# A fused mixer step on Trainium2: the opening of the kernel rewritten as one written order for all engines

## The chip, the cores and the metric

The kernel runs on one core of one Trainium2 chip. The metric is the device time of one execution in microseconds (us), lower is better. The engines of the core run side by side, each with its own queue: PE multiplies matrices, DVE (VectorE) and ACT (ScalarE) work element by element, POOL (GpSimd) does so more slowly, and SP issues the transfers from memory (DMA).

## The reference, cut to what matters

One layer of a mixer for 1024 prompt tokens and 32 sample tokens, width 1024. Everything that follows the opening hangs on `hn`:

```python
mod = jax.nn.silu(c) @ p['w_ada'] + p['b_ada']
shift, scale, gate = jnp.split(mod, 3, axis=-1)
hn = rmsnorm(x, p['norm_g']) * (1.0 + scale[:, None]) + shift[:, None]
proj = hn @ p['w_in']
lru_x, lru_g, xbc, z, dt_raw = jnp.split(proj, ...)
...
xbc_c, new_buf_ssd = causal_conv(xbc, buf_ssd, p['ssd_conv_w'], p['ssd_conv_b'])
xbc_c = jax.nn.silu(xbc_c).astype(jnp.float32)
xs, Bm, Cm = jnp.split(xbc_c, [D_SSD, D_SSD + SSD_GROUPS * SSD_STATE], axis=-1)
dt = jax.nn.softplus(dt_raw + p['ssd_dt_bias'])
```

Then come a chunked state-space scan over 16 heads, a gated linear recurrence (LRU) of width 1024, an output projection and a last RMS norm. There is a prompt row and a sample row of `c`, so every shift, scale and gate has two columns.

## The kernel before, in words

**Tiling.** Features lie on the 128 partitions and tokens along the free dimension. The tokens form three blocks of 384, 384 and 290 columns; the last holds 256 prompt tokens, 32 sample tokens and two columns that carry the shift. A *unit* is 128 output columns of a weight matrix, all 1024 inputs deep, loaded as 8 k-tiles of 128 x 128 (512 KB). Each fp32 operand of a projection is split into a high and a low part, so that a unit takes three matmuls per k-tile and block: high weight x high h (line 219), high weight x low h (220), low weight x high h (221). That is 24 matmuls per block and 72 per unit. `split_unit` makes the parts of a weight: a cast on ACT (line 95) and a subtraction on DVE (97), once on POOL. Units 24 and 25 are the two groups of B, 26 and 27 those of C, 16 to 23 the eight head pairs of x, 28 to 35 those of z.

**The opening** (lines 272 to 372) makes h and with it the first projections:

- The SP queue loads, in the order `XLOAD`: x in pieces (`x`: four for block 0, two each for blocks 1 and 2), w_ada in single units (`s`), the weights of dt (`w`), units 24 and 25 (`B`, `C` in the order of the string).
- `load_x` squares each piece on ACT (line 170) and adds the squares, on DVE for block 0 and on POOL for blocks 1 and 2 (174, 176). `sum_x` and `token_rstd` sum over the features with matmuls against ones (131), take the root on ACT (135) and invert on DVE (136). `norm_x` spreads the result over the partitions with matmuls against the identity (141), copies it to SBUF (186) and scales x with it: five k-tiles of block 0 on DVE from PSUM (192), all others on POOL (194).
- `ada_unit` multiplies silu(c) with one unit of w_ada (eight fp32 matmuls in four column groups, line 114), copies the row out (115) and `ada_columns` turns rows into columns with the selector `sel` (120). Eight units give the scale (`a`, `c` and Acol in line 302), eight more the shift (`s`, lines 364 to 368).
- `h_new` makes, for each k-tile as soon as x is scaled and Acol is there, the high part of h on ACT (210, the *head*) and the low part on DVE (211, the *tail*).
- PE and SP follow the string `PROG`: `W` is a warm-up matmul on ones (289), `a`, `c`, `r`, `R`, `s` as above, `p` and `q` one k-tile of unit 24 and of unit 25, `d` the dt projection of a block (266). The string holds 33 `W`, 16 `p` and 16 `q`, after the 8 warm-up matmuls of `WARM`. It is followed by the shift, the dt block 2 and the last block of unit 24.

The order of DVE, ACT and POOL in the opening, and that of everything behind it, is chosen by the scheduler of the kernel language from its own timeline.

**Behind the opening.** dt is transposed (382); `b_post(0)` and `b_post(1)` move a unit to SBUF with the shift bias (line 238), convolve it (one ACT pass, line 417, and three DVE passes, 419), apply silu and transpose (515); unit 25's last block is projected in between; `dt_chain` works out the decays and writes them to memory; `c_post` does the same for units 26 and 27 and forms the masked C x B products (527, 531). Then come unit 16 and a loop over eight head pairs with two units each (`ssd_decay` scans on DVE, line 551; `ssd_tokens` 567, 569; `ssd_states` 583, 592; `ssd_diag` with the yd matmuls, 608), the LRU loop and the output projection.

## Time and profile before

| What | us |
|---|---|
| Median of three runs (785.03 to 786.59) | 786.38 |
| The profiled execution | 786.8 |
| Its span, from the first to the last instruction | 785.1 |
| First matmul of a projection (line 219) | 20.39 |
| Last matmul of unit 24 | 75.06 |
| First yd matmul of head pair 0 | 146.31 |

How to read the profile lines. A stretch (`10.00:20.00 ...`) gives its length, then for each engine the us in which it was busy and the number of its instructions, then the granted clock of PE (1.00 is full speed), the busy share of the DMA engines and GB/s. A row in order of time gives the start, the duration, engine, line, operation, the tile written and the tiles read, the count, and in brackets the idle time of the engine before it with what ended it. A grouped row ends in `xcount | busy us, mean ns | idle us before, by what`. A row of waits gives total us, times, longest. PEld is PE's loading of weights, which runs beside its matmuls. The modelled duration of a matmul is longer than the step from one to the next; steps are what counts for PE.

### The profile page before, as it was taken

What the parts mean: (1) busy time and instruction counts of PE and PEld (TensorE: products, weight loads), DVE (VectorE), ACT (ScalarE), POOL (GpSimd) and SP (SyncE); (2) the same over time, 40 slices, a digit from 0 to 9 for tenths busy, and PEclk for the clock granted to TensorE, in tenths of its full rate; (3) what the DMA queues carried; (4) which work ended last, traced back from release to release, by engine and by line L of the source; (5) the groups of instructions that cost most, each with busy time, mean ns of one, the idle gap of its engine ahead of it and who ended that gap; (6) DMA issues with size and microseconds to landing.
All of it is one profiled execution on the core that took longest, in us unless ns stands there. A gap on an engine that the chain in (4) does not pass through costs nothing.

```text
span 785.1 us, 13046 instructions
## 1 busy us (share of the span) xinstructions
PE 761.6 (97%) x5230; PEld 737.0 (94%) x5230; DVE 534.5 (68%) x842; ACT 415.2 (53%) x609; POOL 78.0 (10%) x179
## 2 busy tenths in 40 slices
PE   8899999999999999999999999999999999999994
PEld 7678999989999999998999999999999999999994
DVE  3575966798887787877475566546658897635643
ACT  6553855335244253443578877886777654323430
POOL 3581211001000000000010011101101000000000
PEclk9899999999999999999999999999999999999997
DMA  9920214244433424342212111111153685744831
GB/s 326 395 101 2 78 40 139 88 134 139 137 110 121 147 63 161 116 122 89 78 66 88 43 61 35 54 34 61 31 150 114 191 276 162 236 138 142 262 111 68
DMA packets 40188, 96.32 MB, mean 123 GB/s; under 512 B 4536, under 2 KB 22208, under 8 KB 40128
## 3 DMA queue, kind: packets, MB, share of 16 engines
q1 hardware_dynamic: 40128, 95.50, 37.7%
q8 instruction: 41, 0.67, 0.3%
q14 instruction: 19, 0.16, 0.1%
HBM read 85.53 MB, written 9.95 MB: 122 GB/s over the span
## 4 chain that ended last, share of the span: by engine, by line
PE 80%; DVE 9%; DMA 5%; ACT 2%; issue 2%; POOL 1%; SPq 0%; POOLq 0%; DVEq 0%; ACTq 0%
PE pj L221 16%; PE pj L219 16%; PE pj L220 16%; PE mix L862 6%; PE mix L860 6%; PE mix L861 6%; PE yd L608 2%; PE dS L583 2%; DVE hb L211 2%; DMA M<-dA_d 2%; DVE wlo L97 1%; DMA sraw<-in_w_ada_dram 1%; PE yo L623 1%; DVE M L551 1%; PE gt L744 1%
## 5 line engine op out<-in xcount | busy, mean ns | idle before, releaser
L220 PE MATMUL pj<-hb,whi 128*128 128x384 f32 (+1 forms) x864 | 282.8, 327 | 2.5 <-DVE hb L211 2.5
L219 PE MATMUL pj<-hb,whi 128*128 128x384 f32 (+1 forms) x864 | 284.6, 329 | 0.0
L221 PE MATMUL pj<-hb,wlo 128*128 128x384 f32 (+1 forms) x864 | 282.4, 327 | 1.2 <-POOL wlo L97 1.2
L220 PEld LDWEIGHTS pj<-hb,whi 128*128 128x128 f32 x864 | 163.3, 189 | 4.2 <-DVE hb L211 3.2
L221 PEld LDWEIGHTS pj<-hb,wlo 128*128 128x128 f32 x864 | 163.6, 189 | 3.1 <-POOL wlo L97 1.6
L219 PEld LDWEIGHTS pj<-hb,whi 128*128 128x128 f32 x864 | 162.7, 188 | 3.2 <-issue 2.9
L95 ACT CAST whi<-wraw 128x1024 fp32r<-128x1024 f32 x84 | 88.0, 1048 | 142.3 <-PE pj L220 69.4
L97 DVE TENSOR_TENSOR wlo<-wraw,whi 128x1024 fp32r<-128x1024 f32 x83 | 102.5, 1236 | 59.3 <-ACT whi L95 59.3
L862 PE MATMUL mix<-yt,wlo 128*128 128x324 f32 (+2 forms) x320 | 103.9, 326 | 1.0 <-DVE wlo L97 1.0
L860 PE MATMUL mix<-yt,whi 128*128 128x324 f32 (+2 forms) x320 | 104.1, 325 | 0.0
L861 PE MATMUL mix<-yt,whi 128*128 128x324 f32 (+2 forms) x320 | 103.7, 324 | 0.0
L419 DVE SCALAR_TENSOR_TENSOR u<-raw,par,u 128x1060 f32<-128x1060 f32 x60 | 79.7, 1328 | 1.6 <-ACT u L417 1.1
L862 PEld LDWEIGHTS mix<-yt,wlo 128*128 128x128 f32 x320 | 60.0, 188 | 1.4 <-DVE wlo L97 1.3
L860 PEld LDWEIGHTS mix<-yt,whi 128*128 128x128 f32 x320 | 60.1, 188 | 0.2
L861 PEld LDWEIGHTS mix<-yt,whi 128*128 128x128 f32 x320 | 60.0, 188 | 0.1
L238 ACT ACTIVATE raw<-pj,sb 128x384 f32<-128x384 f32 (+2 forms) x80 | 33.9, 477 | 23.0 <-PE pj L221 13.3
L551 DVE TENSOR_TENSOR_SCAN M<-M,mask 128x1060 f32<-128x1060 f32 x16 | 37.8, 2363 | 11.8 <-DMA M<-dA_d 11.8
L879 DVE SCALAR_TENSOR_TENSOR ot<-mix,gate,xr 128x352 f32<-128x352 f32 (+3 forms) x32 | 14.8, 489 | 25.4 <-PE mix L862 21.5
L405 POOL COPY cso<-raw 128x3 f32<-128x3 f32 x20 | 11.8, 590 | 195.9 <-ACT raw L238 195.9
L211 DVE SCALAR_TENSOR_TENSOR hb<-x,Acol,hb 128x384 fp32r<-128x384 f32 (+2 forms) x32 | 28.0, 925 | 3.8 <-ACT hb L210 3.8
L756 DVE SCALAR_TENSOR_TENSOR r<-a,r 128x1060 f32<-128x1060 f32 x8 | 10.1, 1264 | 28.2 <-ACT r L755 28.2
L554 ACT ACTIVATE M<-M 128x1060 f32<-128x1060 f32 x16 | 17.5, 1091 | 22.2 <-DVE M L551 20.3
(228 smaller groups left out, 1063.5 us busy)
## 6 DMA issues: line engine op xcount, KB each, us to landing
wraw<-in_w_out_dram SPq DMA_DIRECT2D x48, 512.0 KB, 3.6
wraw<-in_w_in_dram SPq DMA_DIRECT2D x36, 512.0 KB, 3.7
M<-dA_d SPq DMA_DIRECT2D x16, 530.0 KB, 4.9
sraw<-in_w_ada_dram SPq DMA_DIRECT2D x16, 512.0 KB, 10.2
E<-E_d SPq DMA_DIRECT2D x16, 265.0 KB, 4.0
yz_d<-y SPq DMA_DIRECT2D x8, 530.0 KB, 4.2
wraw<-in_w_ada_dram SPq DMA_DIRECT2D x8, 512.0 KB, 4.4
x<-in_xh_dram SPq DMA_DIRECT2D x4, 384.0 KB, 4.8
```

The source lines that it names most:

```text
L95: nc.scalar.copy(hi, raw)
L97: eng.tensor_sub(lo, raw, hi.bitcast(F32))
L211: nc.vector.scalar_tensor_tensor(hb[b][:, k, 1, s:e], x[:, s:e], Acol[:, k, w:w + 1], hi.bitcast(F32), op0=OP.mult, op1=OP.subtract)
L219: nc.tensor.matmul(out, lhsT=hi[:, kk, :], rhs=hh, start=(kk == 0), stop=False)
L220: nc.tensor.matmul(out, lhsT=hi[:, kk, :], rhs=hl, start=False, stop=False)
L221: nc.tensor.matmul(out, lhsT=lo[:, kk, :], rhs=hh, start=False, stop=(kk == KT - 1))
L238: nc.scalar.activation(dst[0:P, off + d:off + d + e - s], banks[b][0:P, s:e], func, bias=sb[0:P, w:w + 1])
L419: nc.vector.scalar_tensor_tensor(u, raw[:, k:k + TW], wcol(k), u, op0=OP.mult, op1=OP.add)
L551: nc.vector.tensor_tensor_scan(M, M, mask, 0.0, op0=OP.add, op1=OP.mult)
L860: nc.tensor.matmul(ps, lhsT=w[0][:, k, :], rhs=yh, start=(half == 1 and k == 0), stop=False)
L861: nc.tensor.matmul(ps, lhsT=w[0][:, k, :], rhs=yl, start=False, stop=False)
L862: nc.tensor.matmul(ps, lhsT=w[1][:, k, :], rhs=yh, start=False, stop=(half == 0 and k == KT - 1))
```

## The change

The strings `XLOAD` and `PROG` give way to two lists, and the opening (lines 272 to 372) is rewritten so that SP, PE, ACT, DVE and POOL all follow the written order. The list was found by simulating a list schedule, outside of the kernel.

- Three units (24, 25, 26) go through the opening side by side, k-tile by k-tile: a token `m b k u` multiplies both weight parts of unit u with the head of h (two matmuls), `t b k u` the high part with the tail (one matmul). All three blocks of the three units are done when the opening ends.
- w_ada is loaded and multiplied in pairs of units (`s`), with three buffers of two units where there were six of one.
- All sums of squares (`a`, `f`) and all scaling of x (`x`, from PSUM, two k-tiles at a time) are on DVE. POOL is left with memsets and small copies.
- The other tokens: `z` n warm-up matmuls, `q` squares, `c` sums, `r` root, `v` inverse, `b` spreading, `o` copy of a row pair, `k` columns, `A` Acol (on DVE), `h` head, `l` tail, `H` and `L` the two parts of a weight, `p` parks a finished block in SBUF (ACT) so that its PSUM bank comes free, `d` and `e` half a dt block and its copy, `w` and `W` the parts of the dt weights, `K` and `S` the shift, `D` and `E` dt block 2, `y` finishes a unit: block 2 goes to SBUF with the bias, and DVE adds the bias to the 768 parked columns.
- Behind the opening `b_post` and `c_post` take the finished rows, and unit 27 is projected as before. Its loads and those of unit 16 are issued behind the last load of the opening.

```diff
-WARM = 8
-XP = (4, 2, 2)
-SR = 6
-POOL_K = (3, 5, 6)
-XLOAD = "xxxxsxsCsBssswxsxsxssssssss"
-PROG = ("WWWWWWWWWaWWWWWWraWRWcWaWWWWWWcWWWWqpaWWWaqcaqWp"
-        "aWcqppapqcrqqRppdqprpqsqpRqppssqpqqpsssppqssdq")
+FIRST = (24, 25, 26)
+LOADS = "x00 x02 x04 x06 w s w s w s x10 x14 s d s s s s x20 x24".split()
+PROG = (
+        "z34 q00 q02 a02 q04 a04 q06 H0 a06 f0 L0 c0 s0 r0 v0 b0 o0 H1 k0 x00 A0 L1 h00 z6 s2 A1 l00 h01 m000 "
+        "m001 x02 H2 t000 t001 m010 l01 m011 o2 k2 L2 t010 t011 s4 A2 A3 h02 x04 m002 h03 m020 t002 l02 m021 o4 "
+        "m012 q10 l03 t020 t021 t012 k4 q12 x06 m022 q14 m030 A4 t022 A5 m031 a12 h04 t030 m032 t031 h05 m040 l04 "
+        "t032 q16 m041 a14 s6 w l05 t040 t041 o6 m042 W a16 k6 t042 m050 A6 m051 A7 h06 f1 t050 m052 h07 t051 l06 "
+        "c1 l07 t052 m060 r1 m061 v1 t060 b1 t061 m062 x10 m070 t062 m071 x12 h10 t070 m072 p00 t071 s8 l10 p01 "
+        "h11 x14 m100 m101 o8 t072 h12 t100 l11 t101 s10 p02 l12 h13 x16 m102 o10 m110 m111 q20 l13 t102 t110 q22 "
+        "t111 m112 m120 q24 a22 m121 q26 t112 t120 a24 t121 m122 h14 m130 a26 m131 h15 t122 l14 t130 h16 t131 "
+        "m132 l15 m140 h17 m141 l16 t132 t140 t141 l17 m142 m150 f2 m151 c2 t142 t150 r2 t151 m152 v2 b2 m160 x20 "
+        "m161 t152 t160 x22 t161 h20 m162 m170 x24 h21 m171 s12 x26 h22 t162 s14 l20 o12 h23 l21 m172 o14 t170 "
+        "t171 t172 h24 l22 K d10 d11 e1 d00 d01 e0 p10 l23 p11 l24 p12 h25 S h26 l25 h27 l26 l27 m200 t200 m210 "
+        "t210 m220 t220 m230 t230 m240 t240 m250 t250 m260 t260 m270 t270 y0 D E m201 t201 m211 t211 m221 t221 "
+        "m231 t231 m241 t241 m251 t251 m261 t261 m271 t271 y1 m202 t202 m212 t212 m222 t222 m232 t232 m242 t242 "
+        "m252 t252 m262 t262 m272 t272 y2 "
+).split()
...
+    def scale_x(b, k):
+        w = XB[b][1]
+        x = xin[b][:, k:k + 2, :]
+        nc.vector.tensor_mul(x, x, xbc[b][:, None, 0:w].to_broadcast([128, 2, w]))
...
+    with tc.manual_schedule(engines={E.SP, E.PE, E.Activation, E.DVE, E.Pool}):
...
         def load_next():
+            t = left_loads[0]
+            if t == "s":
+                n = len(sraw)
+                if n >= 3 and 2 * n - 6 not in paired:
                     return False
+                sraw.append(st.tile([128, 2, KT, 128], F32, name="sraw", tag="sraw", bufs=3))
+                u = (2 * n + KT) % (2 * KT)
+                last[0] = dma(sraw[n], a["w_ada"][u:u + 2].rearrange("i p k n -> p i k n"))
+            elif t == "w":
+                ws.append(fetch_unit(a["w_in"][FIRST[len(ws)]]))
+            elif t == "d":
+                dma(wdt, a["w_dt"])
+            else:
+                if t == "x20" and "l07" not in seen:
+                    return False
+                last[0] = load_x(int(t[1]), int(t[2]))
...
+        def mm(u, b, k, heads):
+            w = ws[u]
+            for i in range(2) if heads else (0,):
+                nc.tensor.matmul(banks[u][b], lhsT=w[i][:, k, :], rhs=hb[b][:, k, 0 if heads else 1, :],
+                                 start=(heads and k == 0 and i == 0), stop=(not heads and k == KT - 1))
...
+        def park(u, b):
+            if u not in raws:
+                raws[u] = raw_tile(FIRST[u] - 8, ssd_state(FIRST[u] - 16), ("raw", "raw", "zs")[u])
+            for (s, e, d, w) in EV[b]:
+                nc.scalar.copy(raws[u][:, 3 + d:3 + d + e - s], banks[u][b][:, s:e])
...
+            elif c == "y":
+                sb = shift_bias(banks[n])
+                evacuate(raws[n], 3, AF.Identity, banks[n], 128, (2,), sb)
+                r = raws[n][:, 3:771]
+                nc.vector.tensor_scalar(r, r, sb[:, 0:1], None, op0=OP.add)
+                save_raw(raws[n], FIRST[n] - 8)
+            seen.add(t)
...
-    b_post(0, bk_b0, (0, 1, 2))
-    b_post(1, project(wB[1], (2, 0, 1), bk_b1), (0, 2, 1))
+    b_post(0, raws[0])
+    with tc.issue_after(last[0].ins):
+        banks = project(load_unit(a["w_in"][27]))
+    b_post(1, raws[1])
     dt_chain()
-    for g in range(2):
-        w = load_unit(a["w_in"][26 + g])
-        c_post(g, project(w))
+    c_post(0, raws[2])
+    c_post(1, ssd_raw(banks, 11))
```

## The prediction

> **What bounds the kernel now.** I read the page first: the busy shares, then the slices.

> ```profile
> span 785.1 us, 13046 instructions
> PE 761.6 (97%) x5230; PEld 737.0 (94%) x5230; DVE 534.5 (68%) x842; ACT 415.2 (53%) x609; POOL 78.0 (10%) x179
> ```

> TensorE is the bound: busy 97% of the span. A busy PE need not be doing useful work at full speed, though, so the next view is the stretches of the first 50 us.

> ```profile
> core 0: us, PE busy (x) PEld busy (x) DVE busy (x) ACT busy (x) POOL busy (x), PEclk, DMA share, GB/s
> 0.00:10.00 10.00, 6.99 (x34) 6.79 (x34) 2.55 (x5) 6.25 (x8) 2.15 (x14) 1.00 0.78 244
> 10.00:20.00 10.00, 9.48 (x100) 8.60 (x101) 4.95 (x9) 6.03 (x13) 4.65 (x4) 0.83 1.04 410
> 20.00:30.00 10.00, 8.35 (x79) 6.53 (x78) 4.54 (x5) 4.89 (x13) 5.11 (x3) 0.83 1.06 383
> 30.00:40.00 10.00, 7.88 (x64) 6.26 (x63) 6.63 (x5) 5.95 (x14) 6.23 (x5) 0.83 1.04 407
> ...
> 75.30:146.30 71.00, 71.00 (x484) 69.37 (x485) 54.62 (x109) 43.51 (x68) 10.85 (x36) 1.00 0.25 79
> ```

> Three things stand there. The transfers run at about 0.4 MB/us without a break until 40 us. PE holds few matmuls in these 40 us, and part of them at a granted clock of 0.83. From 75.3 us on PE is never idle. So whatever the opening saves is saved at the end, provided that the stretch after 75 us stays this dense. Next the chain of waits and the order of time, for what delays PE in the opening.

> ```profile
> 7.96 10.78 DMA sraw<-in_w_ada_dram
> ...
> 20.76 2.64 POOL wlo L97
> ...
> 45.15 4.23 DVE hb L211 x2
> ...
> 146.31 1.02 PE yd L608 x16
> ```

> Transfers until 18.7, then GpSimd's split of a weight, then the tails of h on DVE: inputs, not PE. The rows of PE itself, from the order of time:

> ```profile
> 20.39 0.42 PE L219 MATMUL pj<-hb,whi 128*128 128x384 f32 x1
> ...
> 97.51 0.34 PE L219 MATMUL pj<-hb,whi 128*128 128x384 f32 x1
> ...
> 105.99 0.30 PE L219 MATMUL pj<-hb,whi 128*128 128x290 f32 x1
> ...
> 71.97 0.30 PE L219 MATMUL pj<-hb,whi 128*128 128x290 f32 x1
> ...
> 75.06 0.29 PE L221 MATMUL pj<-hb,wlo 128*128 128x290 f32 x1
> ```

> The first projection matmul starts at 20.39. Between 97.51 and 105.99 lie 48 matmuls of 384 columns: 0.1767 us each. Between 71.97 and 75.06 lie 23 steps of 290 columns: 0.134 each. One unit (24 matmuls for each of the three blocks) is thus 48 x 0.1767 + 24 x 0.134 = 8.5 + 3.2 = 11.7 us of PE.

> At 75.2 the kernel before has finished unit 24 and two blocks of unit 25 (16 p, 16 q and the last block in its order). The new opening ends with units 24, 25 and 26 all finished. The same state is reached before at 75.2 + 3.2 + 11.7 = **90.1 us**, since PE is dense there. That is the mark to beat.

> **The change, part by part.** The first stage is set by arrivals.

> ```profile
> 9.14 0.84 ACT L170 ACTIVATE xsq<-x 128x768 f32<-128x768 f32 x1 [0.33 <-DMA x<-in_xh_dram]
> 10.52 0.94 PE L114 MATMUL ada_s<-sraw,sc 128*32 128x128 f32 x16 [2.38 <-DMA sraw<-in_w_ada_dram]
> 14.79 0.64 PE L114 MATMUL ada_s<-sraw,sc 128*32 128x128 f32 x16
> 14.11 0.75 PE L131 MATMUL xcol<-ones,xsq 128*128 128x1 f32 x6
> 15.69 0.83 PE L141 MATMUL xbc<-ident,xrs 128*128 128x128 f32 x6
> 16.58 0.51 PE L120 MATMUL ada_c<-sel,srow 128*128 128x2 f32 x4
> 15.66 1.05 ACT L95 CAST whi<-wraw 128x1024 fp32r<-128x1024 f32 x1
> 107.10 1.23 DVE L97 TENSOR_TENSOR wlo<-wraw,whi 128x1024 fp32r<-128x1024 f32 x1 [2.48 <-ACT whi L95]
> ```

> Summing the GB/s of the stretches, 2.4 MB have moved at 10 us, 6.5 at 20, 10.4 at 30, 14.4 at 40. The first w_ada unit of before, with 2.24 MB up to its end, falls due at 9.5 by this and lands at 10.5, so I add 1.0 to each. The new list loads, in MB up to and including: x of block 0 1.7, w 2.2, pair s0 3.3, w 3.8, pair s2 4.9, w 5.4, pair s4 6.4, x of block 1 8.0, pair s6 9.1, and so on. The pairs land at 13.1, 16.9, 20.8 and 27.6. A pair is 8 matmuls of 256 columns where a unit has 128: between one unit's 0.64 and two units' 1.28; I take 1.1. Then: s0 until 14.2, b0 15.0, k0 15.6. DVE scales two k-tiles from PSUM (2 x 0.55 by the row of one, below) until 16.2, then ACT's head of h until 16.9. PE takes s2 from 16.9 to 18.0, and m000 starts at **18.0**, 2.4 earlier than before. The 34 fp32 warm-up matmuls and z6 fill PE until then and delay nothing but themselves.

> From there PE's own work is the sum:

> ```profile
> 42.94 2.96 PE L266 MATMUL pdt<-hb,wd 128*32 128x384 f32 x16
> 69.82 2.31 PE L266 MATMUL pdt<-hb,wd 128*32 128x290 f32 x16 [0.57 <-DVE hb L367]
> 67.41 1.84 PE L120 MATMUL ada_c<-sel,hrow 128*128 128x2 f32 x16
> ```

> Three units 3 x 11.7 = 35.1; six more pairs 6.6; dt blocks 2 x 2.96 + 2.31 = 8.2; three k of 0.51 and K 1.84 = 3.4; c and b for blocks 1 and 2 about 1.25 + 1.45 = 2.7. Together 56.0: **74.0** with no gap.

> Can the others keep up? The rows of one instruction each:

> ```profile
> L211 DVE SCALAR_TENSOR_TENSOR hb<-x,Acol,hb 128x384 fp32r<-128x384 f32 x16 | 21.0, 1358 | 3.8 <-ACT hb L210 3.8
> 52.43 1.13 DVE L211 SCALAR_TENSOR_TENSOR hb<-x,Acol,hb 128x384 fp32r<-128x384 f32 x2
> 53.93 4.84 POOL L194 TENSOR_TENSOR x<-x,xbs 128x576 f32<-128x576 f32 x3 [2.23 <-ACT xbs L186]
> L192 DVE TENSOR_TENSOR x<-x,xbc 128x384 f32<-128x384 f32 x5 | 2.4, 548 | 0.0
> L174 DVE TENSOR_TENSOR xsq<-xsq 128x768 f32<-128x768 f32 x3 | 2.9, 958 | 3.5 <-ACT xsq L170 3.5
> L210 ACT ACTIVATE hb<-x,Acol 128x384 fp32r<-128x384 f32 x16 | 9.2, 615 | 3.5 <-POOL x L194 3.3 <-DVE x L192 0.2
> ```

> The tail of h (L211) takes 1.36 in the mean but 0.57 each in the pair at 52.43, while GpSimd is idle (2.23 us before its next work at 53.93). GpSimd at work beside it slows it. With GpSimd reduced to memsets and small copies I take 0.57. A block then asks of DVE four scalings (4.4), eight tails (4.6) and the sums of squares of the next block (about 3.4) = 12.4, of ACT eight heads (4.9), four squares (0.84 each by the row at 9.14, 3.4) and copies (2 to 3) = 11, and of PE 12.7 for its nine matmuls per k-tile, plus pairs, c and b. The squares of all blocks, the heads and the parkings are hidden by this PE work, and so are the additions of the shift bias after each unit's last block (y0 to y2: one DVE pass each over 768 columns, under the next unit's matmuls, the last one counted below by starting DVE 1 us late); uncovered, each would cost its own length. PE leads; should L211 stay at 1.36, DVE has 18.8 per block and PE waits some 4 us in each of two blocks.

> Waits that the written order adds. All engines run it in order, so a late input stops everything behind it. (1) s6: the list puts 9.2 us of PE work between 18.0 and s6, plus 0.2 for s4; its data land at 27.6: 0.5 lost. (2) The x of block 2 is queued on SP behind the last pair, which waits for s8 to free its buffer. s8 ends at about 37.3 by the sum. The issue row below gives 3.7 us for 0.52 MB, of which 1.3 are at 0.4 MB/us and 2.4 are start; so 2.4 and 5.6 for the 2.2 MB that follow give 45.3. ACT stands at its squares of that x, the last two (0.7 each) end at 46.7, and only then comes h14, which PE wants at 44.7: 2.0 lost. Behind ACT's wait stand h14 to h17, on which PE's last four k-tiles of block 1 hang. (3) Going back and forth between fp32 and projection matmuls: 1.0, between nothing and the 3.3 us that the two rows of waits show.

> ```profile
> wraw<-in_w_in_dram SPq DMA_DIRECT2D x36, 512.0 KB, 3.7
> ...
> PEld ada_s L114 <- issue: 1.8, 7, 0.4
> ...
> PEld pj L219 <- issue: 1.5, 6, 0.4
> ```

> The opening ends at 74.0 + 0.5 + 2.0 + 1.0 = **77.5**, 12.6 before the mark.

> What of it is given back? First, unit 27 must be split: a cast (1.05) and a subtraction (1.23) that may only be queued behind the opening; the dt transposes cover some of it. Between 0 and 2.3: I take 1.0. Second, DVE. Up to the first yd matmul of head pair 0, at 146.3, DVE has 54.6 us of work after 75.3 (stretch above), 1.2 of it unit 26's subtraction, which moves ahead. It can begin at about 78.5. Were it never idle, it would be done at 131.9; PE, 11.6 ahead, would want it at 134.7. A slack of 2.8 where before had 16.4: the convolutions that used to run beside unit 26 now share a shorter stretch. I take 2.0 lost, between 0 and the rival below.

> Sum: 12.6 - 1.0 - 2.0 = 9.6 faster. The profiled run took 786.8 (its span and 1.7 around it), the median of three is 786.4; from the median: **776.8**.

> **Rivals.** *Clean*: no wait for x, no switching cost, no loss behind: end at 74.5, 15.6 faster, 771. For it: every stall above is mine, and the x arrival hangs on 2 us of margin. *DVE half-bound*: the convolutions, the dt chain and the scans find no order without holes, and DVE idles 9 of its former 16.4 us: 6.2 are lost beyond the slack, 4.2 more than I took: 781. For it: DVE is already the fuller of the small engines, and each head pair leaves it little to catch up with. *Slower, DVE chain*: the 71 us from 75.3 to 146.3 are a chain of dependences and not a lack of input. DVE starting at 78.5 then reaches yd at 149.5, 3.2 later than before: 790. It decides from the point where DVE idles more than 14.4 of its former 16.4 us. Against it: PE was busy 71.00 of 71.00 there, so what DVE waited for was PE's projections, and these come sooner. *Clock*: two rows show what a gap does.

> ```profile
> 20.90:24.30 3.40, 1.83 (x21) 1.22 (x21) 3.40 (x4) 0.88 (x2) 2.49 (x1) 1.00 1.06 392
> 24.30:27.70 3.40, 3.40 (x32) 2.67 (x25) 0.23 (x2) 0.84 (x3) 0.00 (x0) 0.51 1.06 385
> ```

> PE was busy 1.83 of 3.40, and the next 3.4 us had half the clock: 1.7 us of work lost. The 2.0 wait at 44.7, if it falls into one such window, does the same, and three such windows cost 5: 782. [...] *Not what it says*: the part after the opening is planned anew by the scheduler and gives everything back: 786.

> **How the numbers follow.** Forecast 0.46, clean 0.12, DVE half-bound 0.18, clock 0.10, not what it says 0.05, slower 0.09. The range goes from the clean end, 771, to 784.5, which takes in both middle rivals and their sum with the splitting at its worst; some 0.15 is left out. About 0.2% is what a measurement here can tell. Faster 0.46 + 0.12 + 0.18 + 0.10 = 0.86; within 0.2% 0.05; slower 0.09.

> **What would show it.** Right: the first projection matmul near 18; L211 near 0.57 for 384 columns; PE dense from there, one gap of 1 to 3 us near 45; the third unit's last matmul near 77.5; the first yd near 136. Wrong: the clock at half in several stretches of 20 to 55; DVE full from 78 to 130 while PE waits; L211 above 1; m000 after 20.

## The result and the profile after

The changed kernel takes **775.23 us** in the median (773.41 to 775.93, four runs) against 786.24 of the kernel before on the same chip: a ratio of 0.9859, 95% interval 0.9839 to 0.9879, so 11 us faster. The profiled execution took 775.32, its span is 773.6. The forecast was 776.8, with a range from 771.0 to 784.5. (One execution of the kernel before and one of a variant below ran at a granted clock of 0.556 and took over 1230 us; they are left out of every median and ratio.)

The page of the changed kernel opens with the busy shares of the span:

```profile
span 773.6 us, 12733 instructions
...
PE 756.6 (98%) x5100; PEld 730.2 (94%) x5100; DVE 533.2 (69%) x861; ACT 413.3 (53%) x599; POOL 46.7 (6%) x159
```

PE has 130 instructions fewer and is busy 5.0 us less; the span is 11.5 shorter. So more than half of the saving is idle time that has gone, which the shares, 97% and 98%, hardly show. It has to be looked for in the stretches of the opening (columns as before: busy time and number of instructions of each engine, granted clock, DMA share, GB/s):

```profile
core 0: us, PE busy (x) PEld busy (x) DVE busy (x) ACT busy (x) POOL busy (x), PEclk, DMA share, GB/s
17.62:79.55 61.93, 57.97 (x417) 48.64 (x413) 38.41 (x76) 31.32 (x68) 2.30 (x3) 1.00 0.48 177
20.00:50.00 30.00, 26.65 (x192) 22.64 (x193) 19.53 (x36) 16.62 (x31) 0.00 (x0) 1.00 0.84 316
...
83.80:87.20 3.40, 3.40 (x15) 3.40 (x14) 1.73 (x4) 3.37 (x6) 2.13 (x7) 0.50 0.61 178
87.20:146.00 58.80, 58.80 (x413) 55.84 (x413) 47.25 (x111) 30.85 (x48) 5.82 (x20) 1.00 0.25 71
```

The first row is the new opening, from the first projection matmul to the last. Its clock is 1.00 throughout, where before had 0.83 between 10 and 40; PE is idle for 61.93 - 57.97 = 4.0 us of it. In the third row stands a stretch at half clock (0.50 for 3.4 us), behind the opening; the trace, whose record of the clock begins at 5.29, has no other until 766.46, where the last 7 us of the span are at half clock too (in the kernel before the last 10, from 775.31). In the last row PE is never idle, with DVE busy 47.25 of 58.80.

The order of time on PE shows the ends of the opening and its two largest gaps (start, length, engine, line, operation; in brackets the idle time and what ended it):

```profile
17.62 0.45 PE L355 MATMUL pj<-hb,whi 128*128 128x384 f32 x1
...
21.43 1.07 PE L120 MATMUL ada_s<-sraw,sc 128*32 128x256 f32 x16 [0.98 <-DMA sraw<-in_w_ada_dram]
...
45.14 0.33 PE L355 MATMUL pj<-hb,wlo 128*128 128x384 f32 x1
47.76 0.44 PE L355 MATMUL pj<-hb,whi 128*128 128x384 f32 x1 [2.28 <-ACT hb L224]
...
79.42 0.29 PE L355 MATMUL pj<-hb,whi 128*128 128x290 f32 x1
79.55 0.30 PE L236 MATMUL pj<-hb,whi 128*128 128x290 f32 x1
...
80.72 2.12 PE L467 MATMUL dtT<-selD,dtp 32*128 32x16 f32 x18
```

L355 is the line of all three units. The gap at 45 is put down to ACT's head of h; ACT's own rows say why that came late:

```profile
40.23 0.37 ACT L424 COPY hrow<-ada_s 128x256 f32<-128x256 f32 x1 [0.38 <-PE ada_s L120]
44.43 0.69 ACT L179 ACTIVATE xacc<-x 128x576 f32<-128x576 f32 x1 [3.83 <-DMA x<-in_xh_dram]
...
47.10 1.11 ACT L224 ACTIVATE hb<-x,Acol 128x384 fp32r<-128x384 f32 x2
```

ACT stood 3.83 us at the squares of block 2, whose data were not there, and the heads of block 1 stood behind it in the written order. The groups of DVE in the first 80 us:

```profile
L228 DVE SCALAR_TENSOR_TENSOR hb<-x,Acol,hb 128x384 fp32r<-128x384 f32 x16 | 9.4, 615 | 1.0 <-ACT hb L224 0.9
...
L217 DVE TENSOR_TENSOR x<-x,xbc 128x768 f32<-128x768 f32 x8 | 7.5, 949 | 3.4 <-PE xbc L211 3.4
...
L182 DVE TENSOR_TENSOR xacc<-xacc,xsq 128x768 f32<-128x768 f32 x6 | 5.7, 955 | 4.1 <-ACT xsq L179 4.0
```

L228 is the tail of h (L211 before): 615 ns in the mean against 1358. Last, the first yd of head pair 0, at 146.24 before by the order of time:

```profile
134.80 0.43 PE L688 MATMUL yd<-M,xdt 128*64 128x128 f32 x2
```

That is 11.44 earlier, but only two of its 16 matmuls stand there; the other 14 follow at 137.99, the first of them 8.3 ahead of its place before. From the starts of the same groups in both traces the lead is 9.8 at the second pair, 9.2 to 9.4 from the third to the seventh, 10.1 from the eighth pair to the output stage, and 11.5 at the end of the span.

### The profile page after: what moved, and what is told of

The parts are those of the page before. It is cut to its first block, busy times and chain, and to the rows that moved or that the text cites. A ratio compares the mean times of both kernels' runs of the same rounds, so it can differ in the third digit from the quotient of the medians.

```text
span 773.6 us, 12733 instructions
## 1 busy us (share of the span) xinstructions
PE 756.6 (98%) x5100; PEld 730.2 (94%) x5100; DVE 533.2 (69%) x861; ACT 413.3 (53%) x599; POOL 46.7 (6%) x159
## 4 chain that ended last, share of the span: by engine, by line
PE 85%; DVE 6%; DMA 5%; ACT 2%; issue 1%; SPq 1%; POOL 0%; POOLq 0%; DVEq 0%; ACTq 0%
PE pj L236 16%; PE pj L238 16%; PE pj L237 16%; PE mix L943 6%; PE mix L941 6%; PE mix L942 6%; PE pj L355 3%; PE yd L688 2%; PE dS L663 2%; DMA sraw<-in_w_ada_dram 2%; PE yo L703 2%; PE ada_s L120 1%; PE xsT L647 1%; PE gt L825 1%; PE gt L827 1%; PE gt L826 1%
## 5 line engine op out<-in xcount | busy, mean ns | idle before, releaser
L236 PE MATMUL pj<-hb,whi 128*128 128x384 f32 (+1 forms) x792 | 260.1, 328 | 0.0
L237 PE MATMUL pj<-hb,whi 128*128 128x384 f32 (+1 forms) x792 | 259.5, 328 | 0.0
L238 PE MATMUL pj<-hb,wlo 128*128 128x384 f32 (+1 forms) x792 | 259.4, 327 | 0.0
L101 ACT CAST whi<-wraw 128x1024 fp32r<-128x1024 f32 x81 | 84.9, 1048 | 138.1 <-PE mix L942 68.4
L238 PEld LDWEIGHTS pj<-hb,wlo 128*128 128x128 f32 x792 | 150.0, 189 | 1.6 <-issue 1.5
L103 DVE TENSOR_TENSOR wlo<-wraw,whi 128x1024 fp32r<-128x1024 f32 x81 | 98.6, 1219 | 48.0 <-ACT whi L101 48.0
L498 DVE SCALAR_TENSOR_TENSOR u<-raw,par,u 128x1060 f32<-128x1060 f32 x60 | 78.5, 1311 | 1.5 <-ACT u L496 1.1
L255 ACT ACTIVATE raw<-pj,sb 128x256 f32<-128x256 f32 (+1 forms) x74 | 30.9, 468 | 25.4 <-PE pj L238 14.6
L355 PE MATMUL pj<-hb,whi 128*128 128x384 f32 (+1 forms) x144 | 38.5, 339 | 2.5 <-ACT hb L224 2.5
L355 PEld LDWEIGHTS pj<-hb,whi 128*128 128x128 f32 x144 | 25.1, 189 | 7.0 <-ACT hb L224 3.5
L299 POOL COPY cso<-raw 128x3 f32<-128x3 f32 x20 | 15.8, 789 | 230.6 <-ACT raw L255 230.6
## 6 DMA issues: line engine op xcount, KB each, us to landing
wraw<-in_w_out_dram SPq DMA_DIRECT2D x48, 512.0 KB, 3.7
wraw<-in_w_in_dram SPq DMA_DIRECT2D x36, 512.0 KB, 3.7
wraw<-in_w_ada_dram SPq DMA_DIRECT2D x8, 512.0 KB, 5.0
```

The costliest lines, as they stand in the source:

```text
L101: nc.scalar.copy(hi, raw)
L103: eng.tensor_sub(lo, raw, hi.bitcast(F32))
L236: nc.tensor.matmul(out, lhsT=hi[:, kk, :], rhs=hh, start=(kk == 0), stop=False)
L237: nc.tensor.matmul(out, lhsT=hi[:, kk, :], rhs=hl, start=False, stop=False)
L238: nc.tensor.matmul(out, lhsT=lo[:, kk, :], rhs=hh, start=False, stop=(kk == KT - 1))
L255: nc.scalar.activation(dst[0:P, off + d:off + d + e - s], banks[b][0:P, s:e], func, bias=sb[0:P, w:w + 1])
```

## The experiments

Two theories of where the 11 us come from. **Contention**: GpSimd's arithmetic held up DVE's passes, and PE waited for those; without it the same work fits in less time. **Order**: with three units interleaved PE always has a matmul that can run, whatever DVE takes for a pass, and less of the opening is waiting. All times are medians, with the ratio to the kernel before on the same chip (785.97 to 786.24 in the median) and its 95% interval. The runs used three chips or more, so small differences between rows are better read from the ratios (0.001 is 0.8 us).

| kernel | us | ratio |
|---|---|---|
| before, no GpSimd arithmetic | 778.36 | 0.9909 (0.9886 to 0.9931) |
| before, sums of squares on DVE | 779.67 | 0.9924 (0.9903 to 0.9945) |
| before, scaling on DVE | 785.00 | 0.9992 (0.9977 to 1.0007) |
| before, unit 24's low part on DVE | 785.03 | 0.9987 (0.9974 to 1.0000) |
| changed | 775.23 | 0.9859 (0.9839 to 0.9879) |
| changed, two units | 781.96 | 0.9957 (0.9934 to 0.9980) |
| changed, no warm-up | 779.73 | 0.9914 (0.9899 to 0.9929) |
| **changed, x of block 2 early** | **771.67** | 0.9817 (0.9800 to 0.9834) |
| x early, two units | 774.37 | 0.9863 (0.9838 to 0.9889) |
| x early, no warm-up | 773.74 | 0.9841 (0.9819 to 0.9863) |
| x early, w_ada unit by unit | 773.47 | 0.9838 (0.9815 to 0.9861) |
| x early, GpSimd kept busy | 778.16 | 0.9904 (0.9881 to 0.9926) |
| x early, sums of squares on GpSimd | 771.47 | 0.9824 (0.9805 to 0.9842) |

**The kernel before without GpSimd arithmetic.** The old order is kept; scaling, sums and unit 24's low part go to DVE.

```diff
-POOL_K = (3, 5, 6)
+POOL_K = ()
-        eng = nc.gpsimd if b else nc.vector
+        eng = nc.vector
-                nc.gpsimd.tensor_mul(x, x, sb[:, None, :].to_broadcast([128, step, n]))
+            nc.vector.tensor_mul(x, x, bc[:, None, 0:n].to_broadcast([128, step, n]))
-                wB[i] = split_unit(fetch_unit(a["w_in"][24 + i]), eng=(nc.gpsimd, nc.vector)[i])
+                wB[i] = split_unit(fetch_unit(a["w_in"][24 + i]), eng=nc.vector)
```

> The kernel before with one edit: all sums of squares, all scaling of x and the low part of unit 24 on DVE, none on GpSimd; its written order of PE and SP and the scheduler's order of the others stay. Theory (the interleaved order is the main part): the tails of h drop from 1.36 to about 0.6 us each, the waits at 22 and 34 us shrink, and 2 to 4 us of the 11 are gained; 782 to 784. Rival (GpSimd's arithmetic was the main cost): 8 us or more are gained, 778 or less.

It came to 778.36, 7.9 us of the 11, which is the rival's forecast to within 0.4 and not the theory's 2 to 4. The stretch from 20 to 50 of this kernel, and the same of the kernel before:

```profile
20.00:50.00 30.00, 28.38 (x270) 23.42 (x270) 24.78 (x44) 18.65 (x46) 0.37 (x4) 1.00 0.81 300
```

```profile
20.00:50.00 30.00, 26.22 (x213) 21.03 (x212) 17.71 (x15) 15.91 (x38) 20.83 (x14) 0.89 0.75 285
```

DVE does seven microseconds more work than before, and yet PE is busier and the clock is full. So most of the gain can be had in the old order, by taking the arithmetic off GpSimd. This run does not show by itself that held-up passes are the reason: GpSimd's results also came late (in the kernel before PE waits 1.2 us for its low part of unit 24), and the scheduler chooses a new order of ACT and DVE for every such edit.

**Which of the three.** One part of that diff at a time: the sums (`eng = nc.vector`), the low part (the line of `wB[i]`), the scaling (`POOL_K` and the product, and without the copy of the row of factors to SBUF).

> The kernel before with only the sums of squares of blocks 1 and 2 moved from GpSimd (1.4 to 1.8 us each) to DVE (0.96 each). Theory: they stand beside DVE's split of unit 25 (2.61 us instead of 1.23) and the tails of block 0 just ahead of PE's wait of 2.08 us at 34.4 and the half clock behind it, so 2 to 4 us faster than before, 782 to 784. Rival (GpSimd's scaling is what matters): within 1 us of before.

> The kernel before with only the low part of unit 24 moved from GpSimd (2.67 us at 20.7) to DVE. All three of GpSimd's tasks together were worth 7.9 us (before_no_pool). In the trace of before, PE waits 1.24 us for this one at 23.4 and runs 3.4 us at half the clock right behind it. Theory (each wait of PE costs its length and the clock spell behind it): about 3 us faster than before, 783. Rival (another wait is late next): within 1 us of before.

> The kernel before with only the scaling of x moved from GpSimd (three k-tiles of block 0, all of blocks 1 and 2, 2.0 us for two k-tiles) to DVE (0.55 for one, from PSUM). Theory: the tails beside it, 2.1 us each at 45, drop to 0.6 and the heads wait no longer; 2 to 4 us faster than before, 782 to 784. Rival (scaling is most of GpSimd's cost): 5 us or more faster, 781 or less.

The sums of squares of blocks 1 and 2 alone give 6.5 us, more than the 2 to 4 expected; the low part about 1, with an interval that ends at no change, where 3 were expected; the scaling nothing that can be told from zero, against both of its forecasts. The sums as GpSimd's groups in the kernel before:

```profile
L174 POOL TENSOR_TENSOR xsq<-xsq 128x768 f32<-128x768 f32 x3 | 5.5, 1825 | 16.3 <-ACT xsq L170 16.2
...
L174 POOL TENSOR_TENSOR xsq<-xsq 128x576 f32<-128x576 f32 x3 | 4.6, 1520 | 3.7 <-ACT xsq L170 3.6
```

Some 10 us of work, at 1825 ns for 128x768 where DVE takes 958 in the same kernel, none of which shows among PE's waits. DVE in the kernel before, and in the one with only the sums moved, at unit 25's split:

```profile
30.48 2.61 DVE L97 TENSOR_TENSOR wlo<-wraw,whi 128x1024 fp32r<-128x1024 f32 x1 [5.95 <-ACT whi L95]
33.02 4.10 DVE L211 SCALAR_TENSOR_TENSOR hb<-x,Acol,hb 128x384 fp32r<-128x384 f32 x4
```

```profile
25.49 2.02 DVE L174 TENSOR_TENSOR xsq<-xsq 128x768 f32<-128x768 f32 x2 [1.03 <-ACT xsq L170]
27.43 1.22 DVE L97 TENSOR_TENSOR wlo<-wraw,whi 128x1024 fp32r<-128x1024 f32 x1
28.57 0.55 DVE L176 TENSOR_TENSOR xsq<-xsq 128x384 f32<-128x384 f32 x1
29.04 1.14 DVE L211 SCALAR_TENSOR_TENSOR hb<-x,Acol,hb 128x384 fp32r<-128x384 f32 x2
```

The split takes 2.61 beside GpSimd's sums and 1.22 without them; four tails 4.10 or two 1.14. PE in the kernel before waits for exactly this:

```profile
31.92 0.42 PE L219 MATMUL pj<-hb,whi 128*128 128x384 f32 x1
34.42 0.53 PE L220 MATMUL pj<-hb,whi 128*128 128x384 f32 x1 [2.08 <-DVE hb L211]
34.75 0.52 PE L221 MATMUL pj<-hb,wlo 128*128 128x384 f32 x1
```

L220 starts 2.50 after L219, and the 0.33 between the last two starts, where 0.18 is the dense step, shows the half clock that followed. With the sums moved both are gone. The split's extra 1.39 and some 0.7 of the first tail (1.28 of its own instead of 0.57) make up the 2.08 of the wait, and the half clock behind it (0.50 from 34.62 to 38.03) costs another 1.7, half of its 3.4 us. That is not the whole of the 6.5. With the sums moved the split also starts 3.05 earlier, at 27.43: ACT's cast ahead of it begins at 26.24 instead of 29.38, because the scheduler placed ACT's squares differently and because PE, whose w_ada rows ACT copies in between, does not run at half clock from 24.38 to 27.79 as it does before (the granted clock from 20 to 50 is 1.00 with the sums moved and 0.89 before). What these two are worth was not measured apart. The cast in the kernel before, then with the sums moved:

```profile
29.38 1.07 ACT L95 CAST whi<-wraw 128x1024 fp32r<-128x1024 f32 x1
...
26.24 1.06 ACT L95 CAST whi<-wraw 128x1024 fp32r<-128x1024 f32 x1
```

Where only the low part or only the scaling was moved, this wait stayed (2.49 and 2.50 from start to start): another wait was late next.

**The x of block 2 ahead of the last pair.** An edit of the order of the loads alone, in the changed kernel:

```diff
-LOADS = "x00 x02 x04 x06 w s w s w s x10 x14 s d s s s s x20 x24".split()
+LOADS = "x00 x02 x04 x06 w s w s w s x10 x14 s d s s s x20 x24 s".split()
```

> The change with one edit: the two transfers of x for block 2 stand ahead of the last w_ada pair instead of behind it. In the changed kernel PE stands still for 2.4 us at 45.1 because that x lands at 44.4 and 45.9. Theory (the opening's PE time is carried to the end one for one): the gap closes, the span falls by about 2 us, to near 773 from 775.2. Rival (DVE or the transfers behind the opening set the end): the gap closes and the end stays within 0.5 us of the changed kernel.

771.67, 3.6 us less than the changed kernel, and with the last kernel below, which differs from it by less than a run from the next, the fastest of all. The stretches:

```profile
40.00:50.00 10.00, 10.00 (x67) 9.48 (x58) 6.12 (x12) 5.34 (x12) 0.00 (x0) 1.00 0.63 254
50.00:76.40 26.40, 26.15 (x190) 21.29 (x190) 15.37 (x34) 12.73 (x32) 2.22 (x3) 1.00 0.06 21
76.40:90.00 13.60, 13.60 (x93) 13.32 (x92) 12.44 (x20) 12.92 (x20) 7.93 (x17) 1.00 0.27 83
```

PE is busy 10.00 of 10.00 where the gap was, the opening ends at 76.47 instead of 79.55, and from 76.4 to 90 the clock is full. Its lead over the kernel before is 13.2 us at the middle head pairs, against 9.3. The edit touches two loads and nothing else, so it is shown that the wait for x cost time, apart from contention and the third unit. How much is less sure than 3.6: the half-clock stretch behind the opening, 1.7 us (half of 3.4), went too, and no run shows that the edit is what removed it (last section); the two profiled executions differ by 1.9 in span; and the span times the granted clock, an estimate of the time at full clock, is 765.7 against 767.5 in the median. So about the 2 us that were expected belong to the gap.

**Parts of the written order.** The third unit (projected behind the opening instead, with the list thinned of its entries) and the warm-up matmuls (z34 and z6 left out) were each taken away from the changed kernel first:

```diff
-FIRST = (24, 25, 26)
+FIRST = (24, 25)
...
-        banks = project(load_unit(a["w_in"][27]))
+        banks26 = project(load_unit(a["w_in"][26]))
...
-    c_post(0, raws[2])
-    c_post(1, ssd_raw(banks, 11))
+    c_post(0, ssd_raw(banks26, 10))
+    c_post(1, ssd_raw(project(load_unit(a["w_in"][27])), 11))
```

```diff
-        "z34 q00 q02 a02 q04 a04 q06 H0 a06 f0 L0 c0 s0 r0 v0 b0 o0 H1 k0 x00 A0 L1 h00 z6 s2 A1 l00 h01 m000 "
+        "q00 q02 a02 q04 a04 q06 H0 a06 f0 L0 c0 s0 r0 v0 b0 o0 H1 k0 x00 A0 L1 h00 s2 A1 l00 h01 m000 "
```

> The change with two units instead of three side by side; unit 26 is projected behind the opening like unit 27, in one dense piece of 11.7 us. Everything else of the order is kept. Theory (three units are what keeps PE fed in the opening): PE has 6 instead of 9 matmuls per k-tile, 1.06 us against about 1.5 us of DVE per k-tile, and waits some 4 to 6 us in blocks 0 and 1; about 780. Rival (order, pairs and a free GpSimd do it, the third unit is only work moved ahead): within 1 us of the changed kernel.

> The change without its 34 and 6 warm-up matmuls. Theory: PE comes cold to the first sums at 11.4 us and runs c0, s0, b0, k0 and s2 at half the clock (3.4 us of work become 6.8), so the first projection matmul moves from 17.6 to about 19.5 and the first k-tiles run at half as well: 3 to 5 us slower, near 779. Rival (arrivals of the pairs hide it): within 1 us of the changed kernel.

Both lose much, 6.7 and 4.5 us, but the traces show that this is not the price of the part. In each the x of block 2 comes later against PE's work, and the gap at 45 grows, with a half-clock stretch behind it. The kernel with two units:

```profile
39.80:44.60 4.80, 0.41 (x3) 0.09 (x1) 1.73 (x3) 3.05 (x6) 0.00 (x0) 0.85 1.06 411
43.10:53.40 10.30, 8.77 (x30) 8.27 (x31) 7.60 (x14) 5.46 (x13) 0.00 (x0) 0.50 0.43 159
```

The one without warm-up:

```profile
46.40:50.80 4.40, 0.46 (x4) 0.14 (x2) 1.89 (x3) 3.25 (x6) 0.00 (x0) 0.85 0.90 364
49.50:59.70 10.20, 8.97 (x31) 8.65 (x32) 4.54 (x10) 3.10 (x7) 0.00 (x0) 0.50 0.08 33
```

So both were repeated on the kernel with the early x, where no such wait stands:

> Two units side by side (as in two_units) and the x of block 2 loaded ahead of the last w_ada pair (as in x2_early, 771.7). In two_units PE stood still for 4.8 us at 39.9 for that x and then ran 9 us at half the clock, which blurs what the third unit is worth. Theory now (the third unit mainly fills waits; without the wait for x only holes of 1.7 and 0.6 us at 24 to 27 are left): 2 to 4 us above x2_early, 774 to 776. Rival (the third unit itself keeps PE fed all through blocks 0 and 1): the 6.7 us between two_units and the change stay, 778 or more.

> No warm-up matmuls, and the x of block 2 loaded early. In no_warm the wait for x had grown to 4.3 us and was followed by 9 us at half the clock. Theory: with that wait gone, what is left of the missing warm-up is the cold clock until about 22 us: 1 to 3 us above x2_early, 773 to 775. Rival (a cold start delays the whole opening by the 4.5 us measured): 776 or more.

There the third unit is worth 774.37 - 771.67 = 2.7 us and the warm-up 2.1 (by the ratios, since the chip was another one, 3.6 and 1.9; in the traces' leads 2.2 and 2.3). The interval without warm-up overlaps that of the early x, so its price rests on the trace as well: there the matmuls of 384 columns stand 0.32 us apart until 22.2, where the dense step at full clock is 0.18. The pairs of w_ada were undone in the same kernel, two passes of 128 columns for one of 256:

```diff
-        for kk in range(KT):
+        for i in range(n):
+            for kk in range(KT):
...
-            nc.tensor.matmul(ps[q, :], lhsT=sc[:, kk, :], rhs=raw[:, :, kk, :] if n > 1 else raw[:, kk, :],
+                nc.tensor.matmul(ps[q, i * 128:(i + 1) * 128], lhsT=sc[:, kk, :],
+                                 rhs=raw[:, i, kk, :] if n > 1 else raw[:, kk, :], start=(kk < 4), stop=(kk >= 4))
```

> x2_early with each w_ada pair multiplied as two units of 128 columns, loaded and copied as pairs as before. A pair takes PE 1.07 us against 2 x 0.64. Theory (PE's time in the opening comes out at the end): eight pairs x 0.2 = 1.7 us slower, 773.4. Rival (the pairs stand where PE would wait anyway): within 0.5 us of x2_early.

773.47, 1.8 more and close to the theory's number, but the intervals of the two kernels overlap, and the traces do not bear the theory out. Unit 27 begins at 76.09 there, 0.4 sooner than with the pairs; from the first projection matmul on (17.22 against 18.09) the opening is 0.5 longer, not 1.7. Behind it this execution has a half-clock stretch of 3.41 us, from 79.94, which the one with the pairs has not, and that alone is worth 1.7. The lead at the head pairs differs by 0.4. So the pairs are worth about half a microsecond in the opening, and no more is shown.

**GpSimd beside the new order.** Fourteen additions of 768 columns on a tile of zeros, whose result nobody waits for:

```diff
+        noise = st.tile([128, 768], F32, name="noise")
+        nc.gpsimd.memset(noise, 0.0)
+        for i in range(14):
+            nc.gpsimd.tensor_add(noise, noise, noise)
```

> x2_early with work for GpSimd that nobody waits for: 14 additions of 768 columns of a tile of zeros, from about 3 to 30 us. Theory A (GpSimd at work slows DVE's passes over SBUF): the tails of h in block 0 rise from 0.6 to over 1 us, the additions too, and PE waits: 3 to 7 us above x2_early, 775 to 779. Theory B (in the kernel before only the slow and late results of GpSimd cost time): within 1 us of x2_early.

6.5 us slower than without, although nothing depends on them. The groups:

```profile
L321 POOL TENSOR_TENSOR noise<-noise 128x768 f32<-128x768 f32 x14 | 25.5, 1820 | 1.1
...
L228 DVE SCALAR_TENSOR_TENSOR hb<-x,Acol,hb 128x384 fp32r<-128x384 f32 x16 | 10.9, 706 | 0.5 <-ACT hb L224 0.4
...
L182 DVE TENSOR_TENSOR xacc<-xacc,xsq 128x768 f32<-128x768 f32 x6 | 7.7, 1291 | 3.3 <-ACT xsq L179 3.2
L217 DVE TENSOR_TENSOR x<-x,xbc 128x768 f32<-128x768 f32 x8 | 7.5, 947 | 3.8 <-PE xbc L211 3.8
L413 DVE TENSOR_TENSOR wlo<-wraw,whi 128x1024 fp32r<-128x1024 f32 x3 | 6.9, 2296 | 0.0
```

L182, L228 and the split (L413) read two operands from SBUF: 1291, 706 and 2296 ns in the mean (the noise ends at 30.2, and only the first three of the 16 tails, of 1.69, 0.95 and 0.70 us, begin beside it) against 955 and 615 in the changed kernel's rows above, and 1.22 us for such a split in the rows of the kernel with the sums moved. L217 reads one of its two from PSUM: 947 against 949, untouched, and the one that begins at 20.10, beside the noise, takes 0.95 us. So with GpSimd at work the three groups with two SBUF inputs became longer, and the one with an input in PSUM did not; these runs do not show what it is that holds the three up. PE, at the place where it lost:

```profile
10.40:15.20 4.80, 0.33 (x4) 0.14 (x3) 4.66 (x4) 1.63 (x2) 4.57 (x4) 0.98 1.03 422
15.00:25.20 10.20, 10.02 (x60) 7.32 (x60) 7.72 (x9) 3.74 (x6) 9.81 (x6) 0.50 1.04 396
```

The sums of block 0 are on the path that releases the first projection, PE stands idle from 10.4 to 15.2 and works at half clock for the next 10 us. This seemed to settle it for the contention theory. But the noise runs ahead of and beside the first projections, and where PE lost it had nothing else to do yet. So the last run put back what the kernel before had lost most by, the sums of blocks 1 and 2:

```diff
-        nc.vector.tensor_add(xsq[b, 0], xsq[b, 0], xsq[b, k])
+        (nc.gpsimd if b else nc.vector).tensor_add(xsq[b, 0], xsq[b, 0], xsq[b, k])
-        nc.vector.tensor_add(xsq[b, 0][:, 0, :], xsq[b, 0][:, 0, :], xsq[b, 0][:, 1, :])
+        (nc.gpsimd if b else nc.vector).tensor_add(xsq[b, 0][:, 0, :], xsq[b, 0][:, 0, :], xsq[b, 0][:, 1, :])
```

> The kernel is the changed one with the x of block 2 loaded before the last pair, and the eight additions of the sums of squares of blocks 1 and 2 (three passes and a halving for each) put back on GpSimd: the opposite of the run that moved them off it in the kernel before. Theory A, contention: GpSimd's additions take about 1.5 to 1.8 us each as in the kernel before, DVE's passes with two SBUF inputs beside them are held up (splits at 2 us or more, tails of 384 columns at 0.7 or more in the mean), and PE waits for them, with half-clock stretches behind the waits: 2 to 6.5 us slower than 771.7, so 774 to 778. Theory B, the written order has enough room: DVE is relieved of about 3.4 us for each of two blocks, the additions are wanted late, and PE's own work covers the rest: 770.5 to 772.5, and no wait of PE above 1 us that the kernel without this edit does not have.

771.47 against 771.67, and by the ratios 0.0007 more with intervals that overlap: no loss that can be told. The held-up passes are there. Two of DVE's tails in this kernel, the group of all 16, then the engines in the stretch of the two tails:

```profile
27.00 4.39 DVE L228 SCALAR_TENSOR_TENSOR hb<-x,Acol,hb 128x384 fp32r<-128x384 f32 x2 [1.43 <-ACT hb L224]
...
L228 DVE SCALAR_TENSOR_TENSOR hb<-x,Acol,hb 128x384 fp32r<-128x384 f32 x16 | 14.3, 926 | 6.1 <-ACT hb L224 6.1
```

```profile
26.90:31.40 4.50, 4.39 (x36) 3.31 (x35) 4.41 (x3) 1.98 (x5) 4.26 (x4) 1.00 1.01 401
```

Two tails take 4.39 us instead of 1.14, and during that very time PE is busy 4.39 of 4.50: it runs matmuls of the three units on k-tiles that are ready, and a w_ada pair. So the order theory holds in the new kernel, as far as the sums go. The two theories are not rivals but two cures of one wait: in the old order, where PE stood behind one tail, the sums cost 6.5 us by the run above; in the new order they cost nothing that can be told. Not tried: the written order with GpSimd's part of the scaling and of the splits, and so the order alone with everything else as before.

## Why the prediction was right, step by step

- **The mark at 90.1, PE dense from there.** By it the opening, over at 79.55, is 10.5 ahead; 1.7 of that, half of 3.4, go to the half-clock stretch at 83.8 to 87.2, and the traces' lead from the third head pair on is 9.3. The mark is good to about half a microsecond.
- **First projection matmul at 18.0, a pair 1.1.** 17.62 and 1.07. The sum of arrivals held to half a microsecond; the third pair's, 20.8, was 0.6 early, as PE could start it only at 21.43.
- **The opening's end at 77.5.** It was 79.55, 2.0 late; with the DVE backlog below this is the step that failed by most. PE's own 56.0 with 1.0 for switching came to 57.97, so 2.0 lie above the sum; that they are switching between kinds of matmul is an estimate by difference, and no run measures it alone. The idle time was put at 0.5 + 2.0 (the first from 0.2 for s4 and 27.6 - 27.4 for s6, which make 0.4) and is 4.0: the wait for x 2.28 (the heads behind it began at 47.1, forecast 46.7), but s4 cost 0.98 where it was priced at 0.2, and shorter ones the rest. 0.4 earlier at the start, 1.0 more switching, 1.5 more idle: 2.0.
- **Unit 27's split, 1.0.** Nothing. Unit 27's first matmul is at 79.55, right behind the last L355. The scheduler had put its split, and the convolution of unit 24, into the written opening; DVE has both ahead of 79:

```profile
72.23 1.22 DVE L103 TENSOR_TENSOR wlo<-wraw,whi 128x1024 fp32r<-128x1024 f32 x1 [0.27 <-ACT whi L101]
74.14 1.32 DVE L498 SCALAR_TENSOR_TENSOR u<-raw,par,u 128x1060 f32<-128x1060 f32 x1 [0.68 <-ACT u L496]
```

- **The DVE backlog, 2.0.** Nothing, for the same reason: DVE began before 78.5, and PE is busy 58.80 of 58.80 from 87.2 to 146. The rivals on DVE (half-bound, and the slower chain) fall with it.
- **The clock.** The rival wanted three half-clock stretches. There was one, behind the opening, worth 1.7; the gap of 2.28 at 45 did not bring one: the clock was 1.00 from 17.62 to 79.55. The forecast's condition was that the wait falls into one window of 3.4 us. By the steps of the last section the gap, from 45.48 to 47.76, fell across two; that this is what decided is the author's reading and was not shown.
- **L211 at 0.57 without GpSimd.** 0.615, and that GpSimd at work beside DVE lengthens the tails is shown by the noise (1.69, 0.95 and 0.70 us beside it) and by the kernel before without the sums (two in 1.14, where the first took 1.28 with them). What hung on it, that PE would wait some 4 us in each of two blocks "should L211 stay at 1.36", was not borne out as far as it was tried: at 0.93 in the mean, with one pair at 2.2 each, PE waited for none of it. No run has the tails at 1.36 in the new order.
- **The sum.** 2.0 lost in the opening and 1.7 to the clock, 3.0 not given back: 8.9 by these terms, where the forecast had 9.6. The lead of 9.3 in the head pairs fits, and the last 2 us of the 11.5 in span come late, at steps of the kernel before that the changed one does not have or has shorter (0.9 of it at the step of before at 354 us, 0.7 at the one at 626, and 0.7 in the last microseconds, where the clock is half in both). No term of the forecast held these, and no experiment explains them: that the time came within 1.6 us owes something to errors that cancel.

## What to carry to other kernels

When GpSimd shares work with DVE, look at DVE's instructions with two SBUF inputs while GpSimd is at work, not at GpSimd's own busy share: beside the noise the sums of squares took 1291 ns against 955, and in the kernel before 10 us of sums on GpSimd cost 6.5, of which PE's wait behind such instructions was 2.08. Either take the work off GpSimd, or give PE other ready matmuls at that place; for these sums one of the two was enough. And in an order written out by hand, find each instruction that waits for a transfer and ask what stands behind it on its engine: the cheapest gain of this study, 3.6 us in the medians of which about 2 are the wait's, came from two loads moved one place ahead. And before a difference of 1 or 2 us is put down to an edit, look whether one of the two traces has a half-clock stretch that the other has not: the one behind the opening lasted 3.4 us at 0.50, which is 1.7.

## What the runs showed of the hardware

The clock after a gap was not what the trace of before had led to expect. The gap of 2.28 at 45 brought no half clock. Gaps with 3.9 to 4.5 us of idle time (3.94 without warm-up, 4.39 with two units, 4.47 with the noise) were followed by half clock for 10.2 us although PE was busy nearly throughout (10.02 of 10.20 with the noise; with two units dense from 44.6 to 53.4), while steps of 2.5 us, some 2.1 of them idle, in the kernel before and its variants went with 3.4 or 6.8. This row is of the variant with the low part moved; the half clock begins inside a step of 2.49, from 30.77 to 33.26:

```profile
32.10:38.90 6.80, 5.64 (x30) 4.79 (x30) 6.18 (x4) 2.55 (x6) 5.61 (x4) 0.50 1.02 407
```

So a gap of about 4 us cost about 5 us on top of itself (half of 10.2), and to remove it is worth about twice its length, by this estimate. The length of a gap alone does not order these cases: 2.28 us of idle time brought no half clock, and 2.08 did.

The stretch at 83.8 in the changed kernel has no gap ahead of it: PE is busy 3.42 of 3.42 from 80.38 to 83.80. What stands there are 18 small matmuls of 16 columns (L467, from 80.72 to 82.84), which the profile counts as busy PE. The kernel with the early x has the same 18, and its clock stays full until the end of the span is near:

```profile
77.67 2.11 PE L467 MATMUL dtT<-selD,dtp 32*128 32x16 f32 x18
...
758.14:761.55 3.41, 1.54 (x12) 1.28 (x11) 1.18 (x3) 0.47 (x1) 0.00 (x0) 1.00 0.00 0
761.55:764.97 3.42, 2.15 (x11) 1.87 (x10) 0.98 (x4) 0.41 (x2) 0.00 (x0) 0.50 0.00 0
```

So the author's reading is that little PE work within one step brings the half clock, and that a wait of some 2 us, or the 18 small matmuls, bring it or not by where the ticks happen to lie. This is not shown. By busy time it does not come out: PE is busy 1.91 of 3.41 us in the step from 20.97 of the kernel before, and the next step is at half clock; it is busy 1.90 of 3.41 in the step from 46.25 of the changed kernel, and the clock stays full. How little is too little is not worked out here, and no edit tested it; moving only those matmuls was not tried.
